# Attention scores in split float32: the low pieces of the keys used where they arise, in matmuls over 64 rows

## The chip, the cores and the metric

The kernel runs on one core of a Trainium2 chip. The metric is the time of one execution in microseconds (us) of device time; three executions of the kernel before took 1040.53, 1043.62 and 1044.70 us, so its median is 1043.62 us. One execution was also recorded by the profiler, instruction by instruction, and all views below are of that record.

## What is computed

One block of a hybrid encoder over 1024 tokens of width 1024, in float32. A normalised input is projected to two groups of heads of 64 columns each. Group A has 8 query heads that share 2 heads of keys and values, a window of 128 tokens with a slope per head (ALiBi) and a learned sink. Group B has 8 heads with keys and values of their own, each chunk of 64 tokens seeing itself and 8 chunks before, with a bias by clipped distance. Then follow norms, an output projection, a residual and an MLP with squared ReLU.

```python
n = rms_norm(h, norm1_g)
qa, ka, va, qb, kb, vb = split(n @ w_in)
# group A, per head
scores = qa @ ka.T * HEAD_DIM ** -0.5 - slopes * dist
p = softmax_with_sink(scores)
ya = p @ va
# group B, per head
scores = qb @ kb.T * HEAD_DIM ** -0.5 + bias[rel]
yb = softmax(scores) @ vb
h = h + concat(rms_norm(ya), rms_norm(yb)) @ w_out
h = h + square(relu(rms_norm(h) @ w_ff1)) @ w_ff2
out = rms_norm(h)
```

## The kernel before

**Two pieces.** TensorE multiplies float32 operands in a rounded form (float32r). To keep precision, each operand x is split into a high piece (x copied to float32r) and a low piece (x minus the high one). A product is the sum of high x high, high x low and low x high (`mm3`, L200).

**Scores.** A head has 64 columns, so a head's high and low queries fit together in the 128 rows of the array. A query tile Q (`new_q`, L462) holds for one head the high piece in rows 0 to 63 and the low piece in rows 64 to 127. Two key tiles go with it (`new_k`, L465: four for the two heads of a pair): one has the high piece of the keys twice, in the upper and the lower 64 rows, the other the low piece twice. So two matmuls over 128 rows give all four products: Q with the high keys, then Q with the low keys, added up in PSUM (`scores`, L598). A block of 128 queries of group A meets 256 columns of keys, in group B 256, 384, 512 or 640 (640 in two parts of 320 in two banks).

**How the pieces get to their rows.** A projection yields both heads of a pair in one tile, head 0 in rows 0 to 63, head 1 in rows 64 to 127. `place` (L350) for group A and `keys_b` (L398) for group B multiply it by the norm's scale on VectorE into a staging tile of the pool `tst` (three buffers), copy it to the high piece on ScalarE, and take the low piece on GpSimd (`split_l`, L176; on VectorE for the first three projections). Then SyncE issues copies from SBUF to SBUF: for queries one for each piece and head, for keys one for each piece, head and repetition (L380 for A, L423 for B). In group B the low pieces are copied first and the copies come once for all 1024 tokens; in group A they come for each 512.

**Stages.** Up to about 40 us the first weights are loaded and the first projections made. Then the units of group A run: scores, exponentials (VectorE adds the bias and finds the maximum, L622, ScalarE takes the exponential, L623), transposes on TensorE (`pt_A`), and the product with the values (`av_A`). From about 160 us the units of group B follow: scores `S_B`, exponentials (L620, L623), pieces in float16 (`H_B`, L863 and L868), a transposing DMA to `G_B` (L871), and float16 matmuls `av_B`. Between the steps of a unit the remaining projections (`ip_qA`, `ip_kB`, `ip_qB`, `ip_vB`) and the output projection of group A (`op_A`) are put in as fillers. Behind about 400 us comes the MLP in float16 pieces, to which nothing here applies.

**What sets the order.** TensorE's order in the attention is the order of the code (`pe`, L136, ties each matmul to the one before; the numbers A_FILL, B_FILL, NEXT_AT and others say how many filler steps go where). On the other engines a scheduler decides from its own estimate of times, so an edit can move instructions that it does not name. SyncE issues nearly all DMAs, one after the other.

Of the kernel before, what the change touches and what calls it, by code (L numbers as in the profile page):

```python
# [12 lines left out]
AF = mybir.ActivationFunctionType  # L13
ALU = mybir.AluOpType
# [3 lines left out]
P = 128  # L18
SEQ = 1024
# [6 lines left out]
HD = 64  # L26
# [32 lines left out]
def kernel(  # L59
# [29 lines left out]
    nc = tc.nc  # L89
# [7 lines left out]
    def f(ap):  # L97
        return ap.bitcast(F32)

    def page(shape, name, dt=F32R):  # L100
        return main.tile(shape, dt, tag="pg", bufs=NPAGES, name=name)
# [68 lines left out]
    def matmul(*args, **kw):  # L170
        pe(nc.tensor.matmul(*args, **kw))  # L171
# [4 lines left out]
    def split_l(engine, lo, full, hi):  # L176
        return engine.tensor_tensor(lo, full, f(hi), ALU.subtract)  # L177
# [85 lines left out]
    R1 = page([P, SEQ], "R1", F32)  # L263
# [86 lines left out]
    def place(acc, kind, name, dst, t, low_engine, st=None, rest=None):  # L350
        if kind == "v" and name != "vA":
            return values_b(acc, name, dst, t)
        if name[1] == "B":
            return keys_b(acc, kind, name, dst, t, low_engine)
        if st is not None:
            pass
        elif name == "vA":
            st = page([P, 2, HALF], f"ts_{name}_{t}")
        else:
            st = main.tile([P, 2, HALF], F32R, tag="tst", bufs=TST, name=f"ts_{name}_{t}")  # L360
        c = slice(t * HALF, (t + 1) * HALF)
        if kind == "v":
            nc.vector.tensor_tensor(f(st[:, 0]), acc, R1[:, c], ALU.mult)
            return lambda *where: turn_v(st, name, dst, t, *where)
        if kind[0] == "q":
            nc.vector.scalar_tensor_tensor(f(st[:, 1]), acc, HD**-0.5, R1[:, c], ALU.mult, ALU.mult)
        else:
            nc.vector.tensor_tensor(f(st[:, 1]), acc, R1[:, c], ALU.mult)
        nc.scalar.activation(st[:, 0], f(st[:, 1]), AF.Copy)
        split_l(low_engine, st[:, 1], f(st[:, 1]), st[:, 0])  # L370

        def copies(heads):
            for hl in range(2):
                for s in heads:
                    src = f(st[s * HD : (s + 1) * HD, hl])
                    if kind == "q":
                        last = nc.sync.dma_start(f(dst[s][hl * HD : (hl + 1) * HD, c]), src)
                    else:
                        for rep in range(2):
                            last = nc.sync.dma_start(f(dst[2 * hl + s][rep * HD : (rep + 1) * HD, c]), src)  # L380
            return last.ins.name

        if rest is None:
            return copies(range(2))
        rest.append(lambda: copies((1,)))
        return copies((0,))

# [5 lines left out]
        nc.scalar.activation(hi, tp, AF.Copy)  # L393
        split_l(nc.vector, dst[t][:, :, :, HD:], tp, hi)

    halves = {}

    def keys_b(acc, kind, name, dst, t, low_engine):  # L398

        if t == 0:  # L400
            halves[name] = [main.tile([P, SEQ], F32R, tag="tst", bufs=TST, name=f"t{hl}_{name}") for hl in (1, 0)]
        c = slice(t * HALF, (t + 1) * HALF)
        lo, hi = (v[:, c] for v in halves[name])
        if kind == "q":
            nc.vector.scalar_tensor_tensor(f(lo), acc, HD**-0.5, R1[:, c], ALU.mult, ALU.mult)
        else:
            nc.vector.tensor_tensor(f(lo), acc, R1[:, c], ALU.mult)  # L407
        nc.scalar.activation(hi, f(lo), AF.Copy)
        split_l(low_engine, lo, f(lo), hi)
        split = name == "qB3"  # L410
        if t == 0 or not split:
            if t == 0 and not split:
                return
            dst.extend(new_q(name) if kind == "q" else new_k(name))
        c = c if split else slice(0, SEQ)
        for hl, v in zip((1, 0), halves[name]):
            for s in range(2):
                src = f(v[s * HD : (s + 1) * HD, c])
                if kind == "q":
                    nc.sync.dma_start(f(dst[s][hl * HD : (hl + 1) * HD, c]), src)  # L420
                else:
                    for rep in range(2):
                        nc.sync.dma_start(f(dst[2 * hl + s][rep * HD : (rep + 1) * HD]), src)  # L423

    def values_b(acc, name, dst, t):

# [35 lines left out]
    def new_q(name):  # L462
        return [page([P, SEQ], f"Q{name}{s}") for s in range(2)]

    def new_k(name):  # L465

        return [page([P, SEQ], f"K{name}{s}") for s in range(4)]

    def new_v(name):
        return [page([P, 4, 2, 2 * HD], f"V{name}{t}") for t in range(2)]  # L470
# [30 lines left out]
    KA, VA, Q = new_k("A"), new_v("A"), new_q("A0")  # L501
# [70 lines left out]
    at = ap_.enter_context(tc.tile_pool(name="at", bufs=1, reuse_waits="tile"))  # L572
# [22 lines left out]
        nb = min(i, 1 if kind == "A" else 4) + 1  # L595
        return i - nb + 1, nb * P

    def scores(kind, i, Q, K, S):  # L598
        k0, n = window(kind, i)
        if n > 512:  # L600
            parts = [(S[:, 0, :320], 0, 320), (S[:, 1, :320], 320, 320)]
        else:
            w = max(n, 2 * P)
            parts = [(S[:, 0, :w], 0, w)]
        for hl in range(2):
            for dst, o, w in parts:
                matmul(
                    dst, Q[:, i * P : (i + 1) * P], K[hl][:, k0 * P + o : k0 * P + o + w],
                    start=hl == 0, stop=hl == 1,
                )  # L610

# [113 lines left out]
    class UnitA:  # L725
# [10 lines left out]
        def score(self, s):  # L736
            p, j = self.pair, self.pair.j
            if s == 0:
                self.nm, self.sm, self.rc = stats(self.name)
            S = group_ps[1].tile([P, 2, 2 * P], F32, tag="S", bufs=2, name=f"S_{self.name}_{s}")  # L740
            pt = tile_of_a(f"P_{self.name}_{s}")
            h = 2 * j + s
            for b in range(2):
                scores("A", self.i0 + b, p.Q[s], p.K[j // 2 :: 2], S[:, b : b + 1])
            for b in range(2):
                c = slice(2 * s + b, 2 * s + b + 1)
                self.P[b, s] = exponentials(
                    "A", self.i0 + b, p.biases()[s], nsink[:, h : h + 1],
                    S[:, b : b + 1], pt[:, b * 2 * P : (b + 1) * 2 * P], self.nm[:, c], self.sm[:, c],
                )  # L750
            if s == 0:
                return
            es = small.tile([P, 4], F32, tag="es", bufs=2, name=f"es_{self.name}")
            for s in range(2):
                c = slice(2 * s, 2 * s + 2)
                nc.scalar.activation(es[:, c], self.nm[:, c], AF.Exp, bias=psink[:, 2 * j + s : 2 * j + s + 1])
            nc.vector.tensor_tensor(self.sm, self.sm, es, ALU.add)
            nc.vector.reciprocal(self.rc, self.sm)
            for (b, s), (k0, n, q) in self.P.items():
                engine = nc.gpsimd if (b, s) in POOL_NORM else nc.vector  # L760
                engine.tensor_scalar(q[:, :n], q[:, :n], self.rc[:, 2 * s + b : 2 * s + b + 1], None, ALU.mult)
# [45 lines left out]
    class UnitB:  # L807
# [10 lines left out]
        def score(self, b):  # L818
            p, h = self.pair, self.h
            if b == 0:  # L820
                self.nm, self.sm, self.rc = stats(self.name)
                banks_of_b()
                pool, cols = (pool_of_b(), 40) if self.t else (at, 20)
                self.G = pool.tile([P, cols, P], F16, tag=f"T16_{self.t}", bufs=2, name=f"G_{self.name}")
            c = slice(b, b + 1)
            S = group_ps[1].tile([P, 2, 512], F32, tag="S", bufs=2, name=f"S_{self.name}_{b}")
            pt = at.tile([P, 5 * P], F32, tag="P", bufs=3, name=f"P_{self.name}_{b}")
            scores("B", self.i0 + b, p.Q[self.s], p.K[self.s :: 2], S)
            if defer:
                defer.pop(0)[1]()  # L830
            self.P[b] = exponentials("B", self.i0 + b, p.biases()[self.s], BIG, S, pt, self.nm[:, c], self.sm[:, c])
            if defer:
                defer.pop(0)[1]()
            if b % 2:
                self.next_bias(b == 1)
            if b % 2:
                H = at.tile([P, 20 * P], F16, tag="P16", bufs=3, name=f"H_{self.name}_{b}")
                defer.append((self, lambda: self.upper(b - 1, H)))
                defer.append((self, lambda: self.lower(b - 1, H)))
# [237 lines left out]
    for j in range(4):  # L1077
        Q, K, V = [], [], []
        fill.add(f"B{j}", in_proj(KB0 + j * P, "k", f"kB{j}", K, None))
        q, v = (QB0 + j * P, "q", f"qB{j}", Q, None), (VB0 + j * P, "v", f"vB{j}", V, None)  # L1080
# [156 lines left out]
    rows = {}  # L1237
# [20 lines left out]
    X, F, S = {}, {}, {}  # L1258
# [402 lines left out]
    acc = {}  # L1661
# [117 lines left out]
    for at, (g, p, n) in enumerate(order2[:-GQ]):  # L1779
# [10 lines left out]
        if g == 0 and step in (4, 7, 10):  # L1790
            last = NQ // GQ - 1
# [21 lines left out]
    g, p, n0 = order2[-GQ]  # L1813
# [104 lines left out]
```

## Time and profile before

| | before |
|---|---|
| median of three executions | 1043.62 us |
| the profiled execution | 1040.53 us |
| its span, first to last instruction | 1038.7 us |
| its mean granted TensorE clock | 0.990 |
| TensorE busy (PE) | 1000.8 us, 4818 matmuls |
| weight loads (PEld) | 591.8 us |
| VectorE (DVE) / ScalarE (ACT) / GpSimd (POOL) busy | 742.5 / 692.6 / 443.9 us |
| DMA | 200.63 MB |

How to read the lines: L171 is line 171 of the kernel; all matmuls have the line of a helper (L171, transposes L174), so they are told apart by the tiles, written out<-in. `128*128` behind a matmul is the part of the array that it uses, `128x512 f32` the shape of its output; `x192` counts instructions. Loads of weights (PEld) overlap matmuls (PE). The end of a matmul is modelled, so the distance from one start to the next says more than a duration. In the lists of waits the numbers are the total in us, how often, and the longest.

### The profile page before, as it was taken

The numbers are of one execution on the slowest core, as the hardware profiler recorded it, in microseconds if no ns is written. First come the engines' busy times: TensorE is split into PE (matmuls) and PEld (weight loads), VectorE is DVE, ScalarE is ACT, GpSimd is POOL, SyncE is SP. The second block draws the span as 40 slices with busy tenths as digits, with TensorE's granted clock in tenths as the row PEclk, the third lists the DMA queues.
The fourth block names the chain that finished last, engine by engine and source line by source line (L and its number), as shares of the span: only waits on it lengthen the run. The fifth ranks groups of instructions, "written<-read, shape, count | busy, mean of one in ns | idle before, by whom it ended". The sixth has DMA issues, their size and how long they took to land.

```text
span 1038.7 us, 14057 instructions
## 1 busy us (share of the span) xinstructions
PE 1000.8 (96%) x4818; PEld 591.8 (57%) x4818; DVE 742.5 (71%) x1259; ACT 692.6 (67%) x1102; POOL 443.9 (43%) x341
## 2 busy tenths in 40 slices
PE   9999999999979999899999999999899999999997
PEld 7878887777757678544444444444344444444443
DVE  6566777867586748994676667664798776786776
ACT  8666766667577736675867865964777765567346
POOL 0456665242453562105245425434255343345333
PEclk9999999999989999989999999999999999999999
DMA  9944438999999885105678668648699545433004
GB/s 353 254 133 133 129 82 184 194 209 225 209 257 251 207 261 182 62 21 166 211 282 293 205 210 274 195 170 310 257 329 388 189 150 186 159 121 122 1 1 162
DMA packets 150567, 200.63 MB, mean 193 GB/s; under 512 B 78688, under 2 KB 96224, under 8 KB 150496
## 3 DMA queue, kind: packets, MB, share of 16 engines
q1 hardware_dynamic: 150352, 199.47, 63.6%
q8 instruction: 38, 0.62, 0.3%
q14 instruction: 33, 0.27, 0.1%
q10 hardware_dynamic: 144, 0.26, 0.1%
HBM read 120.01 MB, written 42.99 MB: 157 GB/s over the span
## 4 chain that ended last, share of the span: by engine, by line
PE 34%; ACT 8%; issue 7%; DMA 7%; DVE 6%; POOL 2%; SPq 1%; DVEq 0%; POOLq 0%; ACTq 0%
PE f_a L171 13%; PE f_c L171 7%; PE f L171 6%; PE f_b L171 4%; DMA w<-in_w_ff_dram 3%; PE op_B L171 2%; ACT w L1362 2%; DMA m<-in_w_ff_dram 2%; DMA u<-ud 2%; POOL W L1397 2%; ACT k L1459 1%; ACT k L1458 1%; ACT W L1395 1%; DMA G_B<-H_B 1%; ACT m L1176 1%
## 5 line engine op out<-in xcount | busy, mean ns | idle before, releaser
L171 PE MATMUL f<-X,W 128*128 128x512 f16 x1344 | 295.3, 381 | 6.6 <-POOL W L1397 5.0
L171 PEld LDWEIGHTS <-U 128*128 128x128 f16 x1356 | 133.0, 98 | 163.9 <-issue 7.2
L171 PEld LDWEIGHTS <-W 128*128 128x128 f16 x1344 | 131.4, 98 | 166.3 <-POOL W L1397 8.2
L1397 POOL TENSOR_TENSOR U<-u,U 128x1024 f16<-128x1024 f32 x48 | 117.3, 2454 | 170.5 <-ACT U L1395 155.2
L171 PE MATMUL f_a<-V,U 128*128 128x512 f16 x756 | 165.3, 379 | 1.0 <-DVE C L1711 1.0
L1397 POOL TENSOR_TENSOR W<-T,W 128x1024 f16<-128x1024 f32 x29 | 69.7, 2407 | 84.3 <-ACT W L1395 84.3
L1397 POOL TENSOR_TENSOR W<-w,W 128x1024 f16<-128x1024 f32 x21 | 51.6, 2458 | 98.6 <-ACT W L1395 98.6
L171 PE MATMUL f_c<-V,U 128*128 128x512 f16 x384 | 86.0, 384 | 3.5 <-DVE V L1399 2.2
L1393 ACT ACTIVATE u<-u,uup 128x1024 f32<-128x1024 f32 x48 | 53.9, 1141 | 53.1 <-DMA u<-ud 53.0
L1399 DVE SCALAR_TENSOR_TENSOR V<-Z,up,V 128x1024 f16<-128x1024 f32 x32 | 51.3, 1605 | 28.7 <-ACT V L1395 20.7
L1395 ACT ACTIVATE U<-u 128x1024 f16<-128x1024 f32 x48 | 50.2, 1046 | 28.1 <-DVE Z L1369 10.4
L623 ACT ACTIVATE P_B<-P_B,nm_B 128x640 f32<-128x640 f32 (+2 forms) x64 | 44.2, 691 | 32.2 <-DVE nm_B L620 16.6
L171 PE MATMUL op_A<-w_o,y 128*128 128x512 f32 x192 | 58.0, 428 | 4.1 <-DVE ts_vB L433 3.9
L868 DVE SCALAR_TENSOR_TENSOR H_B<-P_B,rc_B,H_B 128x640 f16<-128x640 f32 (+2 forms) x64 | 51.0, 825 | 13.6 <-ACT H_B L863 13.3
L1399 DVE SCALAR_TENSOR_TENSOR V<-w,up,V 128x1024 f16<-128x1024 f32 x24 | 42.2, 1756 | 18.0 <-ACT V L1395 13.8
L171 PE MATMUL ip_qB<-nT,w_qB 128*128 128x512 f32 x192 | 53.7, 406 | 1.1 <-DVE t_kB L407 1.0
L171 PE MATMUL ip_kB<-nT,w_kB 128*128 128x512 f32 x192 | 53.7, 405 | 0.0
L1457 DVE CUSTOM_DVE_ANT_0 k<-f,k 128x1024 f32<-128x1024 f32 x24 | 29.3, 1220 | 31.3 <-PE f L171 22.4
L171 PE MATMUL ip_vB<-nT,w_vB 128*128 128x512 f32 x192 | 51.3, 400 | 0.0
L1395 ACT ACTIVATE V<-Z,up 128x1024 f16<-128x1024 f32 x32 | 36.4, 1138 | 22.2 <-DVE Z L1369 19.3
L171 PE MATMUL ip_qA<-nT,w_qA 128*128 128x512 f32 x192 | 50.7, 398 | 0.3 <-DVE VA L177 0.3
L863 ACT ACTIVATE H_B<-P_B,rc_B 128x640 f16<-128x640 f32 (+2 forms) x64 | 40.8, 685 | 9.5 <-DVE rc_B L860 4.2
(284 smaller groups left out, 1980.1 us busy)
## 6 DMA issues: line engine op xcount, KB each, us to landing
w<-in_w_ff_dram SPq DMA_DIRECT2D x64, 512.0 KB, 7.5
u<-ud SPq DMA_DIRECT2D x56, 512.0 KB, 5.4
ud<-k SPq DMA_DIRECT2D x48, 512.0 KB, 3.1
m<-in_w_ff_dram SPq DMA_DIRECT2D x32, 512.0 KB, 5.8
KkB<-t_kB SPq DMA_DIRECT2D x32, 256.0 KB, 5.0
xr<-in_x_dram SPq DMA_DIRECT2D x8, 512.0 KB, 8.8
st_o<-in_w_out_dram SPq DMA_DIRECT2D x8, 512.0 KB, 4.8
h<-in_x_dram SPq DMA_DIRECT2D x8, 512.0 KB, 4.9
```

Of the source, the lines that this page charges most:

```text
L171: pe(nc.tensor.matmul(*args, **kw))
L623: nc.scalar.activation(pr, pr, AF.Exp, bias=nm, scale=-1.0, accum_out=sm)
L863: nc.scalar.activation(hi, q, AF.Copy, scale=rc)
L868: nc.vector.scalar_tensor_tensor(lo, q, rc, hi, ALU.mult, ALU.subtract)
L1176: nc.scalar.activation(src, src, AF.Square, accum_out=self.column())
L1362: nc.scalar.activation(w, w, AF.Copy, scale=up1)
L1393: nc.scalar.activation(full, full, AF.Copy, scale=up)
L1395: nc.scalar.activation(w[0], full, AF.Copy, scale=1.0 if up is None else up)
L1397: engine.tensor_tensor(w[1], full, w[0], ALU.subtract)
L1399: engine.scalar_tensor_tensor(w[1], full, up, w[0], ALU.mult, ALU.subtract)
L1457: dve.tensor_tensor_reduce(v, ps, v, 1.0, 0.0, ALU.add, ALU.max, top)
L1458: nc.scalar.activation(v, v, AF.Relu, scale=down1[n])
```

## The change

The low pieces of the keys are no longer copied. In group A and group B alike the engine that splits writes the low piece straight into a page of its own (`KAl`, `KkB0l` and so on), in which it stands as the projection left it: head 0 (or key head 0) in rows 0 to 63, head 1 in rows 64 to 127. The high pieces are still copied twice for each head. A pair now has three key tiles instead of four (`new_k` returns the low one twice, for the indexing).

The first score matmul stays: 128 rows, queries of both pieces with the high keys. The second is cut to the 64 rows in which the head's low keys lie (`rows` in `scores`, from `half`, which is the key head in group A and the head of the pair in group B). For that the high queries must lie in the same 64 rows: where the half is 1, the query tile now has the low piece in the upper and the high piece in the lower rows (`at = (hl ^ kv) * HD`, `(hl ^ s) * HD`). The product of low queries with low keys is no longer computed. All else stays as it is, the numbers that set the order among it.

```diff
+        hi, raw = st[:, 0], st[:, 1]
+        lo = dst[2][:, c] if kind == "k" else raw
...
+        split_l(low_engine, lo, f(raw), hi)
...
+                if kind == "q":
+                    kv = int(name[2:]) // 2
+                    for hl, src in enumerate((hi, lo)):
+                        at = (hl ^ kv) * HD
+                        last = nc.sync.dma_start(f(dst[s][at : at + HD, c]), f(src[rows]))
+                else:
+                    for rep in range(2):
+                        last = nc.sync.dma_start(f(dst[s][rep * HD : (rep + 1) * HD, c]), f(hi[rows]))
...
-        split_l(low_engine, lo, f(lo), hi)
+        if kind == "k" and t == 0:
+            low_k[name] = page([P, SEQ], f"K{name}l")
+        split_l(low_engine, low_k[name][:, c] if kind == "k" else lo, f(lo), hi)
...
-        for hl, v in zip((1, 0), halves[name]):
+        for hl, v in list(zip((1, 0), halves[name]))[kind == "k" :]:
...
-                        nc.sync.dma_start(f(dst[2 * hl + s][rep * HD : (rep + 1) * HD]), src)
+                        nc.sync.dma_start(f(dst[s][rep * HD : (rep + 1) * HD]), src)
...
-        return [page([P, SEQ], f"K{name}{s}") for s in range(4)]
+        if lo is None:
+            lo = page([P, SEQ], f"K{name}l")
+        return [page([P, SEQ], f"K{name}{s}") for s in range(2)] + [lo, lo]
...
         for hl in range(2):
             for dst, o, w in parts:
+                rows = slice(half * HD, (half + 1) * HD) if hl else slice(0, P)
                 matmul(
-                    dst, Q[:, i * P : (i + 1) * P], K[hl][:, k0 * P + o : k0 * P + o + w],
+                    dst, Q[rows, i * P : (i + 1) * P], K[hl][rows, k0 * P + o : k0 * P + o + w],
                     start=hl == 0, stop=hl == 1,
                 )
```

TensorE's order is the same in both kernels. The first scores of group A, on TensorE, right behind the first projections, stand like this in the kernel before (`KA_197` holds high keys, `KA_199` low ones):

```order
L171 MATMUL ip_vA_427<-nT_192,w_vA 128x512
L171 MATMUL S_A_0_0_592<-KA_197,QA_203 128x256
L171 MATMUL S_A_0_0_592<-KA_199,QA_203 128x256
L171 MATMUL S_A_0_0_592<-KA_197,QA_203 128x256
L171 MATMUL S_A_0_0_592<-KA_199,QA_203 128x256
L171 MATMUL ip_qA_0_611<-nT_181,w_qA_505 128x512
```

The same place on TensorE in the changed kernel, with `KA_198` for the high and `KAl` for the low keys:

```order
L171 MATMUL ip_vA_426<-nT_192,w_vA 128x512
L171 MATMUL S_A_0_0_583<-KA_198,QA_202 128x256
L171 MATMUL S_A_0_0_583<-KAl,QA_202 128x256
L171 MATMUL S_A_0_0_583<-KA_198,QA_202 128x256
L171 MATMUL S_A_0_0_583<-KAl,QA_202 128x256
L171 MATMUL ip_qA_0_602<-nT_181,w_qA_500 128x512
```

Nothing moved; the two matmuls with `KAl` now work on 64 rows, each between two that work on 128.

On SyncE, the queue of DMAs, the key copies of the first pair of group B stand like this before (`KkB_1417` and `KkB_1418` high, `KkB_1419` and `KkB_1420` low; `st_vB` is a weight load, `b_A` a bias, `ya` an output):

```order
L423 DMA KkB_1419<-t_kB_1324 64x1024 x2
L423 DMA KkB_1420<-t_kB_1324 64x1024 x2
L423 DMA KkB_1417<-t_kB_1325 64x1024 x2
L423 DMA KkB_1418<-t_kB_1325 64x1024 x2
L682 DMA ya<-Y_1_1365 128x512
L657 DMA b_A_1699<-in_dist_dram 128x256
L657 DMA b_A_1702<-in_dist_dram 128x256
L127 DMA st_vB_2099<-in_w_in_dram 128x1024
```

The same place on SyncE in the changed kernel, where lines from 382 on have numbers a few higher:

```order
L430 DMA KkB_1409<-t_kB_1316 64x1024 x2
L430 DMA KkB_1410<-t_kB_1316 64x1024 x2
L692 DMA ya<-Y_1_1357 128x512
L127 DMA st_vB_2080<-in_w_in_dram 128x1024
L667 DMA b_A_1685<-in_dist_dram 128x256
L667 DMA b_A_1688<-in_dist_dram 128x256
```

The four low copies are gone, and the weight load stands two places earlier.

On VectorE, in group B where the last projection of values (`ts_vB`) is taken out of PSUM while TensorE goes on to the output projection `op_A`, before:

```order
L405 SCALAR_TENSOR_TENSOR t_qB_3317<-ip_qB_1_3449,R_180 128x512
L917 SCALAR_TENSOR_TENSOR y_1_3403<-y_1_3403,ogc 128x512
L917 SCALAR_TENSOR_TENSOR y_2_3405<-y_2_3405,ogc 128x512
L868 SCALAR_TENSOR_TENSOR H_B_1_1_3490<-P_B_1_0_3458,rc_B_1_3455,H_B_1_1_3490 128x640
L868 SCALAR_TENSOR_TENSOR H_B_1_1_3490<-P_B_1_1_3482,rc_B_1_3455,H_B_1_1_3490 128x640
L620 ISA P_B_1_3_3538,nm_B_1_3453<-S_B_1_3_3537,b_B_587 128x640
L620 ISA nm_B_1_3453 128x1
L917 SCALAR_TENSOR_TENSOR y_3_3407<-y_3_3407,ogc 128x512
L908 TENSOR_TENSOR Y_0_3472<-av_B_0_3494,Y_0_3472 64x512
L433 TENSOR_TENSOR ts_vB_3399<-ip_vB_1_3548,R_180 128x512
```

The same place on VectorE in the changed kernel:

```order
L409 SCALAR_TENSOR_TENSOR t_qB_3288<-ip_qB_1_3420,R_180 128x512
L927 SCALAR_TENSOR_TENSOR y_2_3376<-y_2_3376,ogc 128x512
L927 SCALAR_TENSOR_TENSOR y_3_3378<-y_3_3378,ogc 128x512
L869 TENSOR_SCALAR sm_B_1_3425<-sm_B_1_3425 128x2
L870 RECIPROCAL rc_B_1_3426<-sm_B_1_3425 128x2
L918 TENSOR_TENSOR Y_0_3443<-av_B_0_3465,Y_0_3443 64x512
L878 SCALAR_TENSOR_TENSOR H_B_1_1_3461<-P_B_1_0_3429,rc_B_1_3426,H_B_1_1_3461 128x640
L440 TENSOR_TENSOR ts_vB_3370<-ip_vB_1_3519,R_180 128x512
L878 SCALAR_TENSOR_TENSOR H_B_1_1_3461<-P_B_1_1_3453,rc_B_1_3426,H_B_1_1_3461 128x640
```

`ts_vB` now stands ahead of the second `H_B` and of the score reduction (L620), and behind `Y` as before; on ScalarE `Y` (L907) keeps its place behind `t_qB`, and the two copies that make the high pieces of `H_B` moved behind it.

More of the change, by code (lines that the diff above doesn't have):

```diff
@@ L364, in place @@
             return lambda *where: turn_v(st, name, dst, t, *where)
-        if kind[0] == "q":
-            nc.vector.scalar_tensor_tensor(f(st[:, 1]), acc, HD**-0.5, R1[:, c], ALU.mult, ALU.mult)
-        else:
-            nc.vector.tensor_tensor(f(st[:, 1]), acc, R1[:, c], ALU.mult)
-        nc.scalar.activation(st[:, 0], f(st[:, 1]), AF.Copy)
-        split_l(low_engine, st[:, 1], f(st[:, 1]), st[:, 0])
+        hi, raw = st[:, 0], st[:, 1]
+        lo = dst[2][:, c] if kind == "k" else raw
+        if kind == "q":
+            nc.vector.scalar_tensor_tensor(f(raw), acc, HD**-0.5, R1[:, c], ALU.mult, ALU.mult)
+        else:
+            nc.vector.tensor_tensor(f(raw), acc, R1[:, c], ALU.mult)
+        nc.scalar.activation(hi, f(raw), AF.Copy)
+        split_l(low_engine, lo, f(raw), hi)
         def copies(heads):
[L373 to L380, printed above, removed]
+            for s in heads:
+                rows = slice(s * HD, (s + 1) * HD)
+                if kind == "q":
+                    kv = int(name[2:]) // 2
[5 more added lines that the diff above has]
+                        last = nc.sync.dma_start(f(dst[s][rep * HD : (rep + 1) * HD, c]), f(hi[rows]))
             return last.ins.name
@@ L394, in turn_v @@
         split_l(nc.vector, dst[t][:, :, :, HD:], tp, hi)
-    halves = {}
+    halves, low_k = {}, {}
     def keys_b(acc, kind, name, dst, t, low_engine):
@@ L413, in keys_b @@
                 return
-            dst.extend(new_q(name) if kind == "q" else new_k(name))
+            dst.extend(new_q(name) if kind == "q" else new_k(name, low_k[name]))
         c = c if split else slice(0, SEQ)
-        for hl, v in zip((1, 0), halves[name]):
+        for hl, v in list(zip((1, 0), halves[name]))[kind == "k" :]:
             for s in range(2):
@@ L419, in keys_b @@
                 if kind == "q":
-                    nc.sync.dma_start(f(dst[s][hl * HD : (hl + 1) * HD, c]), src)
+                    at = (hl ^ s) * HD
+                    nc.sync.dma_start(f(dst[s][at : at + HD, c]), src)
                 else:
                     for rep in range(2):
-                        nc.sync.dma_start(f(dst[2 * hl + s][rep * HD : (rep + 1) * HD]), src)
+                        nc.sync.dma_start(f(dst[s][rep * HD : (rep + 1) * HD]), src)
     def values_b(acc, name, dst, t):
@@ L463, in new_q, with new_k @@
         return [page([P, SEQ], f"Q{name}{s}") for s in range(2)]
-    def new_k(name):
-        return [page([P, SEQ], f"K{name}{s}") for s in range(4)]
+    def new_k(name, lo=None):
+        if lo is None:
+            lo = page([P, SEQ], f"K{name}l")
+        return [page([P, SEQ], f"K{name}{s}") for s in range(2)] + [lo, lo]
     def new_v(name):
@@ L596, in window, with scores @@
         return i - nb + 1, nb * P
-    def scores(kind, i, Q, K, S):
+    def scores(kind, i, Q, K, S, half):
         k0, n = window(kind, i)
@@ L743, in score @@
             for b in range(2):
-                scores("A", self.i0 + b, p.Q[s], p.K[j // 2 :: 2], S[:, b : b + 1])
+                scores("A", self.i0 + b, p.Q[s], p.K[j // 2 :: 2], S[:, b : b + 1], j // 2)
             for b in range(2):
@@ L827, in score @@
             pt = at.tile([P, 5 * P], F32, tag="P", bufs=3, name=f"P_{self.name}_{b}")
-            scores("B", self.i0 + b, p.Q[self.s], p.K[self.s :: 2], S)
+            scores("B", self.i0 + b, p.Q[self.s], p.K[self.s :: 2], S, self.s)
             if defer:
```

## The prediction

> **What bounds the kernel now.** I read the page first: who is busy, and in which slices the DMA engines are full.
>
> ```profile
> PE 1000.8 (96%) x4818; PEld 591.8 (57%) x4818; DVE 742.5 (71%) x1259; ACT 692.6 (67%) x1102; POOL 443.9 (43%) x341
> PE   9999999999979999899999999999899999999997
> DMA  9944438999999885105678668648699545433004
> ```
>
> TensorE is busy for 96% of the span. The score matmuls lie between about 40 and 355 us, slices 2 to 14 of 40 (26 us each). In slices 7 to 14 DMA stands at 8 or 9, so copies could matter there. Three windows over this stretch say how much of it TensorE waits.
>
> ```profile
> 60.00:150.00 90.00, 89.97 (x504) 76.50 (x503) 67.09 (x209) 61.75 (x183) 60.57 (x64) 1.00 0.43 118
> 150.00:250.00 100.00, 96.58 (x508) 75.48 (x508) 76.78 (x185) 68.61 (x143) 43.11 (x63) 1.00 0.90 191
> 250.00:360.00 110.00, 102.17 (x503) 74.61 (x502) 80.00 (x172) 77.85 (x152) 46.59 (x50) 0.97 0.98 228
> ```
>
> The columns are the stretch, its length, then PE, PEld, DVE, ACT and POOL busy, clock, DMA share, GB/s. While group A is computed TensorE is idle for 0.03 us of 90. While group B is computed it is idle for 3.4 and 7.8 us, with DMA at 0.90 and 0.98. The waits of TensorE in 150 to 250 (first four) and 250 to 350 us name what ends these gaps.
>
> ```profile
> PE S_B L171 <- DVE nm_B L622: 1.4, 1, 1.4
> PE ip_qB L171 <- DVE t_kB L407: 1.0, 1, 1.0
> PE pt_A L174 <- DVE T_A L177: 0.6, 1, 0.6
> PE av_A L171 <- DVE T_A L177: 0.3, 1, 0.3
> PE op_A L171 <- DVE ts_vB L433: 3.9, 1, 3.9
> PE S_B L171 <- DVE nm_B L620: 3.7, 4, 1.7
> ```
>
> Every one is a wait for VectorE, none for a key copy. So the stretch is bounded by TensorE, then by VectorE's order, and what the change does to a matmul counts nearly one for one.
>
> **Part 1: fewer copies.** Of the key copies half go.
>
> ```profile
> KkB<-t_kB SPq DMA_DIRECT2D x32, 256.0 KB, 5.0
> KA<-ts_kA SPq DMA_DIRECT2D x16, 128.0 KB, 4.8
> ACT t_qB L408 <- DMA KkB<-t_kB: 4.2, 2, 3.5
> SPq L423 <- POOL t_kB L177: 18.5, 3, 14.0
> ```
>
> 16 transfers of 256 KB and 8 of 128 KB are no longer issued. Their relief: ScalarE's two waits for a copy to free the staging tile (4.2 us in all) can go, since that tile is now free as soon as GpSimd has split it. SyncE no longer waits 18.5 us for GpSimd's low pieces, with bias loads, weight loads and transposes queued behind. But no TensorE wait above has a copy at its end. Bounds: nothing, or at most the 11 us of waits listed. I take 0 for the copies, as ScalarE and SyncE have slack here.
>
> **Part 2: the order on VectorE.** The one long gap is the 3.9 us ahead of op_A at 301 to 305 us. It costs more than itself, because the clock falls after it:
>
> ```profile
> 304.00:308.00 4.00, 2.87 (x7) 2.29 (x8) 3.63 (x12) 2.73 (x7) 3.87 (x7) 0.51 1.20 234
> 308.00:312.00 4.00, 4.00 (x17) 2.94 (x16) 2.93 (x5) 2.46 (x5) 3.22 (x5) 0.63 0.87 239
> 300.20 1.67 DVE L868 SCALAR_TENSOR_TENSOR H_B<-P_B,rc_B,H_B 128x640 f16<-128x640 f32 x2
> ...
> 303.67 0.69 DVE L908 TENSOR_TENSOR Y<-av_B,Y 64x512 f32<-64x512 f32 x1 [0.28 <-ACT Y L907]
> 304.38 0.69 DVE L433 TENSOR_TENSOR ts_vB<-ip_vB,R 128x512 f32<-128x512 f32 x1
> ```
>
> At 0.51 and 0.63 the lost work is 0.49 x 2.87 + 0.37 x 4.0 = 2.9 us, so gap and clock are worth 6.8 us. In the changed order (third place shown above) ts_vB stands ahead of the second H_B and the score reduction, but still behind Y, and Y still waits for ScalarE; one H_B now comes between. So it may start some tenths earlier or up to 0.9 us later (one H_B, 1.67 us for two before). Bounds -6.8 to +0.9; I take 0.
>
> The other waits for VectorE (nm_B 1.4 and 3.7, T_A 0.9) shrink if TensorE gets slower, as its results are then due later: -3 us if it does, 0 if not.
>
> **Part 3: the score matmuls over 64 rows.** How many there are, and what one lasts:
>
> ```profile
> L171 PEld LDWEIGHTS S_A<-KA,QqA x96: 187/189/192, 69.5 to 154.7; 128*128 128x128 f32 x96
> L171 PE MATMUL S_A<-KA,QqA x96: 278/282/364, 69.5 to 154.8; 128*128 128x256 f32 x96
> L171 PE MATMUL S_A<-KA,QA x32: 274/282/364, 40.1 to 64.7; 128*128 128x256 f32 x32
> L171 PE MATMUL S_B<-KkB,QqB x192: 277/309/524, 159.8 to 351.8; 128*128 128x320 f32 x128, 128*128 128x256 f32 x32, 128*128 128x384 f32 x16, 128*128 128x512 f32 x16
> ```
>
> Of 128 in A and 192 in B every second one (64 + 96 = 160) becomes a 64-row one, over as many columns as before, so nothing is saved by streaming. The 64 of A stand singly between 128-row ones (hi, lo, hi, lo). In B a row block of up to 512 columns has one low matmul and one of 640 has two together: 64/2 + 128/4 = 64 excursions. Together 128 excursions to 64 rows and back, that is 256 changes of tile size. Every row above has the tile 128*128: no row of this trace shows a change. Its cost is the whole question.
>
> What a matmul costs when its load is hidden, and when it isn't:
>
> ```profile
> 374.45 8.45 PE op_B L171 x36
> 382.91 1.68 PE ss_B L171 x16
> 71.90 0.64 PE L171 MATMUL S_A<-KA,QqA 128*128 128x256 f32 x4
> 72.38 0.86 PE L171 MATMUL ip_qA<-nT,w_qA 128*128 128x512 f32 x3
> ```
>
> 36 matmuls of 512 columns in 8.45 us are 235 ns each, 0.46 ns a column, though each has its own load, and a load of this size lasts 189 ns in the rows above: the loads run beside the streaming. Four S_A take 72.38 - 71.90 = 0.48 us, 120 ns each, and 256 x 0.46 is 118: hidden too. The ss_B matmuls stream one column each, so their 1.68 / 16 = 105 ns is the price of a load with nothing to hide behind.
>
> Below nothing: a hidden load can't be hidden better, 120 against 118 ns, so a gain is excluded. Lower end, the nearest thing to a change of mode, from f32 to f16 and back at the apply matmuls:
>
> ```profile
> 314.99 0.61 PE L171 MATMUL av_B<-G_B,VvB 128*128 128x512 f16 x2
> 315.25 1.05 PE L171 MATMUL op_A<-w_o,y 128*128 128x512 f32 x3
> 316.14 0.50 PE L171 MATMUL av_B<-G_B,VvB 128*128 128x384 f16 x2
> 316.34 0.99 PE L171 MATMUL op_A<-w_o,y 128*128 128x512 f32 x3
> 317.17 0.39 PE L171 MATMUL av_B<-G_B,VvB 128*128 128x256 f16 x2
> 317.17 0.11 PEld L171 LDWEIGHTS <-VvB 128*128 128x128 f16 x2 [0.28 <-issue]
> ```
>
> From av_B to av_B are 1.15 and 1.03 us. Three op_A are 0.705, two av_B of 512 or 384 columns at 0.46 ns are 0.47 or 0.35: the sums, 1.18 and 1.06, even exceed what was measured. The load is held back (0.28 us idle, "issue"), and it costs nothing. So the lower end is 0. Upper end: at each change the matmul before must end (277 - 118 = 159 ns of tail behind its streaming), and only then the load runs (188 ns): 0.35 us, x 256 = 89 us.
>
> Between 0 and 89 us I take the price of an unhidden load, 105 ns a change: weights for another tile size can't be put in place beside a matmul that still uses the whole array, while the tail may overlap the load. 256 x 0.105 = 27 us. This is nearest to the ss_B row, since there too an f32 load of 128 columns has nothing beside it. The f16 row is further off: its array stays 128*128 and its loads are half as long (0.11 us for two). The Trainium skill, TensorEngine Tiling (Array Packing), Tiling Modes, says that changing the tiling mode, not only the tile, drains TensorE; that speaks against this change, and no run here shows it yet. With the 128 cycles of array depth at 2.4 GHz that the Trainium skill, TensorE: Matmul & The Clock Gate, Part 2 (DRAIN), gives, a drain alone would be 53 ns a change, 14 us in all, an estimate from that page; the sum would then be 1054.
>
> **The sum.** The profiled execution took 1040.53 us (span 1038.7); it is the lowest of three, and their median of 1043.62 is 3.1 above. 1040.5 + 27 + 0 + 0 - 3 = 1064.5, on the median 1067.6, given as 1067.
>
> **Rivals.** First, the other side: a change of tile size costs nothing, as that of type does. For it speak the av_B rows; against it, that there the tile stays whole. Then only parts 1 and 2 are left, -6.8 to +0.9, and the median would be about 1042 (1036.8 to 1044.5). It decides from an excursion under (5.2 + 3) / 128 = 64 ns. Second, full serialisation: tail and load in a row at every change, 1043.6 + 89 - 3 = 1130. For it speaks that a reconfigured array may have to be empty before a load; against it, that held-back loads cost nothing at av_B. Halfway between forecast and this lies 1099.
>
> **Chances.** Half a per cent, 5.2 us, is about what can be told from no change here. Forecast 0.49, with its own range 1050 to 1090; free changes 0.31; full serialisation or most of it 0.20. Of the free case a good third, 0.11, has the gap of part 2 closed and is faster by more than 5.2 us; the other 0.20 is no change. All else, 0.69, is slower. The range: down to 1037 takes in nearly all of the free case; up to 1108 half of the serial case. About 0.12 is left out.
>
> **What would show it.** In the changed profile the S rows split into 128*128 and 64*128. Right: an S_A group takes 0.48 + 4 x 0.105 = 0.9 us to the next matmul, PEld shows idle "issue" time ahead of S loads, DMA in slices 7 to 14 falls by some 16 transfers and no TensorE wait for a copy appears. Wrong low: S_A groups still take 0.48 to 0.56 us. Wrong high: S_A groups take 1.5 us or more. Wrong in another way: the time changes behind 400 us, where nothing of this change runs, or the 64-row matmul itself streams slower than 0.46 ns a column.

## The result, and the profile after

The changed kernel took 1081.83 us (median of four executions, 1078.41 to 1083.22) against 1042.07 us before (median of four executions, the three given above among them): 39.8 us more, a ratio of 1.038 with a 95% interval of 1.0357 to 1.0402. Its profiled execution took 1083.22 us with a span of 1081.4, 42.7 us above the span of before.

The page of the changed kernel, the rows that were shown of before:

```profile
PE 1049.8 (97%) x4818; PEld 601.5 (56%) x4818; DVE 744.8 (69%) x1259; ACT 694.5 (64%) x1102; POOL 446.9 (41%) x341
PE   9999999999999999989999998999979999999997
DMA  9833323686999987411676786675799734543004
```

The number of matmuls is the same, and no other engine does clearly more than before: VectorE, ScalarE and GpSimd are busy for 2 to 3 us more. TensorE alone is busy for 49 us more. DMA in slices 3 to 6, with most of group A, falls (3, 3, 3, 2 where 4, 4, 4, 3 stood).

Where TensorE waits, by stages (columns as before: stretch, length, then PE, PEld, DVE, ACT, POOL busy, clock, DMA, GB/s), and its waits in 150 to 400 us:

```profile
60.00:150.00 90.00, 90.00 (x422) 69.15 (x420) 53.72 (x169) 51.83 (x152) 51.15 (x53) 1.00 0.32 85
150.00:250.00 100.00, 97.23 (x434) 68.37 (x434) 69.72 (x183) 60.94 (x143) 39.31 (x45) 0.98 0.60 131
250.00:400.00 150.00, 146.83 (x671) 99.16 (x670) 103.11 (x219) 99.55 (x189) 62.86 (x78) 0.99 0.88 198
```

```profile
PE S_B L171 <- DVE nm_B L632: 2.2, 2, 1.6
PE op_A L171 <- ACT o L1074: 1.7, 1, 1.7
PE ip_qB L171 <- DVE t_kB L411: 0.9, 1, 0.9
PE S_B L171 <- DVE nm_B L630: 0.9, 1, 0.9
PE pt_A L174 <- DVE T_A L177: 0.3, 1, 0.3
```

In the first stage TensorE now does 422 matmuls in 90 us instead of 504, and is busy all the time. The gap of 3.9 us ahead of op_A is gone from the list. So the loss isn't waiting: it sits inside what the profile counts as busy.

The rows of the scores, in the view of the tiles S_A and S_B of the changed kernel:

```profile
L171 PE MATMUL S_A<-KA,QqA x48: 279/373/387, 73.5 to 176.3; 128*128 128x256 f32 x48
L171 PE MATMUL S_A<-KAl,QqA x48: 378/381/383, 73.8 to 176.6; 64*128 64x256 f32 x48
L171 PEld LDWEIGHTS S_A<-KAl,QqA x48: 182/183/183, 73.8 to 176.6; 64*128 64x128 f32 x48
L171 PE MATMUL S_B<-KkB,QqB x96: 276/309/532, 181.4 to 391.7; 128*128 128x320 f32 x64, 128*128 128x256 f32 x16, 128*128 128x384 f32 x8, 128*128 128x512 f32 x8
```

Behind "to" stands the start of the last one. The last S_A started at 154.8 us before and at 176.3 or 176.6 now: 21.8 us later. The last S_B with high keys starts at 391.7; before, the last S_B of all started at 351.8, so some 40 us have come together there. From there to the end only 2 to 3 us are added. Nearly the whole loss arises between the first and the last score, about half in each group.

How, one group of each kind shows. First the timeline of TensorE (start, length as modelled), then its weight loads at the same place:

```profile
73.49 0.36 PE L171 MATMUL S_A<-KA,QqA 128*128 128x256 f32 x1
73.79 0.38 PE L171 MATMUL S_A<-KAl,QqA 64*128 64x256 f32 x1
74.10 0.39 PE L171 MATMUL S_A<-KA,QqA 128*128 128x256 f32 x1
74.41 0.38 PE L171 MATMUL S_A<-KAl,QqA 64*128 64x256 f32 x1
74.72 1.65 PE L171 MATMUL ip_qA<-nT,w_qA 128*128 128x512 f32 x6
...
236.25 0.49 PE L171 MATMUL S_B<-KkB,QqB 128*128 128x512 f32 x1 [1.60 <-DVE nm_B L632]
236.67 0.49 PE L171 MATMUL S_B<-KkB1l,QqB 64*128 64x512 f32 x1
237.09 1.36 PE L171 MATMUL ip_kB<-nT,w_kB 128*128 128x512 f32 x3
```

```profile
73.47 0.19 PEld L171 LDWEIGHTS S_A<-KA,QqA 128*128 128x128 f32 x1
73.78 0.18 PEld L171 LDWEIGHTS S_A<-KAl,QqA 64*128 64x128 f32 x1
74.09 0.19 PEld L171 LDWEIGHTS S_A<-KA,QqA 128*128 128x128 f32 x1
74.41 0.18 PEld L171 LDWEIGHTS S_A<-KAl,QqA 64*128 64x128 f32 x1
```

The four S_A start 0.31 us apart instead of 0.12, and each load starts together with its matmul instead of ahead of it. With 256 columns the step is 0.31 us, with 512 it is 0.42: 0.11 us for 256 columns more, which is their streaming, and a constant of about 0.19 us, which is the length of one load (0.18 to 0.19). So at each change of size the load begins when the streaming before has ended, and lies bare.

### The profile page after: what moved, and what is told of

The parts are those of the page before. It is cut to its first block, busy times and chain, and to the rows that moved or that the text cites. A ratio compares the mean times of both kernels' runs of the same rounds, so it can differ in the third digit from the quotient of the medians.

```text
span 1081.4 us, 14022 instructions
## 1 busy us (share of the span) xinstructions
PE 1049.8 (97%) x4818; PEld 601.5 (56%) x4818; DVE 744.8 (69%) x1259; ACT 694.5 (64%) x1102; POOL 446.9 (41%) x341
## 2 busy tenths in 40 slices
DMA packets 148647, 195.38 MB, mean 181 GB/s; under 512 B 78304, under 2 KB 95840, under 8 KB 148576
## 4 chain that ended last, share of the span: by engine, by line
PE 68%; ACT 10%; DVE 8%; DMA 8%; issue 4%; SPq 1%; POOL 1%; DVEq 0%; ACTq 0%; POOLq 0%
PE f_a L171 13%; PE f L171 7%; PE f_c L171 7%; PE ip_qB L171 4%; PE ip_vB L171 4%; PE ip_kB L171 4%; PE ip_qA L171 4%; PE f_b L171 4%; PE op_A L171 4%; PE S_B L171 4%; DMA w<-in_w_ff_dram 4%; PE S_A L171 3%; PE av_B L171 2%; ACT w L1372 2%; DMA m<-in_w_ff_dram 2%
## 5 line engine op out<-in xcount | busy, mean ns | idle before, releaser
L1409 DVE SCALAR_TENSOR_TENSOR V<-Z,up,V 128x1024 f16<-128x1024 f32 x32 | 48.4, 1511 | 28.3 <-ACT V L1405 18.2
L878 DVE SCALAR_TENSOR_TENSOR H_B<-P_B,rc_B,H_B 128x640 f16<-128x640 f32 (+2 forms) x64 | 49.0, 789 | 16.2 <-ACT H_B L873 15.8
L171 PE MATMUL ip_qB<-nT,w_qB 128*128 128x512 f32 x192 | 56.9, 424 | 0.9 <-DVE t_kB L411 0.9
L171 PE MATMUL ip_kB<-nT,w_kB 128*128 128x512 f32 x192 | 56.7, 422 | 0.0
L633 ACT ACTIVATE P_A<-P_A,nm_A 128x256 f32<-128x256 f32 (+1 forms) x64 | 31.3, 490 | 38.5 <-DVE nm_A L632 37.5
L632 DVE CUSTOM_DVE_ANT_0 P_A<-S_A,b_A,nsink 128x256 f32<-128x256 f32 (+1 forms) x64 | 27.4, 465 | 33.8 <-PE S_A L171 32.1
```

The costliest lines, as they stand in the source:

```text
L632: nc.vector.tensor_tensor_reduce(pr, S[:, 0, :n], bs, -1.0, init, ALU.add, ALU.min, nm)
L633: nc.scalar.activation(pr, pr, AF.Exp, bias=nm, scale=-1.0, accum_out=sm)
L878: nc.vector.scalar_tensor_tensor(lo, q, rc, hi, ALU.mult, ALU.subtract)
L1409: engine.scalar_tensor_tensor(w[1], full, up, w[0], ALU.mult, ALU.subtract)
```

## The experiments

Three theories were tested. Theory 1: a change of tile size holds the next load back. Theory 2: a matmul over 64 rows is itself slow. Theory 3: the moved instructions and the low keys' new path cost the time. The first four kernels were measured together; the kernel before took 1040.38 us beside them. On every engine the instructions of the first and the fourth stand in the order of the changed kernel, those of the second in the order of before. An excursion is a change to 64 rows and back.

**Without the 64 rows.** The edit, in `scores` of the changed kernel:

```diff
-                rows = slice(half * HD, (half + 1) * HD) if hl else slice(0, P)
+                rows = slice(0, P)
```

> The changed kernel with its second score matmul over all 128 rows again, still on the uncopied low keys; copies and the order on every engine are those of the changed kernel. (It adds the low queries of a head times the low keys of the other head, a term of the size of the one that the change leaves out.) Theory 1, a change of tile size holds back the next load, 0.19 us each way: no change of size is left, so the 39.8 us go and the time is 1042 us, within 4 us either way for the fewer copies and the new order. Theory 2, a matmul over 64 rows is itself slow: the same, 1042 us. Theory 3, the moved instructions and the low keys' new path cost the time: it stays near 1082 us.

Measured: 1041.92 us, ratio 1.001 (0.9994 to 1.0027). The whole loss is gone, with half of the key copies gone as well. Theory 3 falls. The tile S_A in this kernel, and its waits of TensorE from 290 to 330 us:

```profile
L171 PE MATMUL S_A<-KAl,QqA x48: 278/281/284, 68.3 to 152.9; 128*128 128x256 f32 x48
```

```profile
PE op_A L171 <- DVE ts_vB L440: 4.3, 1, 4.3
PE op_A L171 <- ACT o L1074: 3.0, 1, 3.0
PE S_B L171 <- DVE nm_B L630: 0.7, 1, 0.7
```

The last S_A starts within 2 us of before. The gap ahead of op_A is 4.3 us, 0.4 more than the 3.9 of before: the new place of ts_vB on VectorE doesn't shorten it. The removed copies and the new order together gain nothing that can be measured; this kernel has both, so a small gain of one and a small loss of the other aren't told apart.

**Only the 64 rows.** The kernel before, copies and all:

```diff
             for dst, o, w in parts:
+                rows = slice(0, HD) if hl else slice(0, P)
                 matmul(
-                    dst, Q[:, i * P : (i + 1) * P], K[hl][:, k0 * P + o : k0 * P + o + w],
+                    dst, Q[rows, i * P : (i + 1) * P], K[hl][rows, k0 * P + o : k0 * P + o + w],
```

> The kernel before with its copies and its order, only the second score matmul cut to rows 0 to 63 (high queries; the product of low queries and low keys is left out). Theory 1: 256 changes of size, so as slow as the changed kernel, 1080 to 1090 us, the start-to-start distances of S_A near 0.31 us instead of 0.12. Theory 2: the same. Theory 3: as fast as before, 1042 us.

Measured: 1077.61 us, ratio 1.0361 (1.0334 to 1.0388), 37.2 us slower (34.7 to 40.4, which takes in the 39.8). This one part makes the loss. Its timeline has the four S_A in one row:

```profile
68.08 1.21 PE L171 MATMUL S_A<-KA,QA 128*128 128x256 f32 x4
69.22 1.65 PE L171 MATMUL ip_qA<-nT,w_qA 128*128 128x512 f32 x6
```

They take 69.22 - 68.08 = 1.14 us, where four took 0.48 before (72.38 - 71.90).

**As many matmuls over 64 rows, fewer changes.** In group A both high matmuls first, then both low ones:

```diff
-    def scores(kind, i, Q, K, S, half):
+    def scores(kind, i, Q, K, S, half, pieces=range(2)):
...
-        for hl in range(2):
+        for hl in pieces:
...
-                    start=hl == 0, stop=hl == 1,
+                    start=hl == 0, stop=hl == 1, skip_group_check=kind == "A",
...
-            for b in range(2):
-                scores("A", self.i0 + b, p.Q[s], p.K[j // 2 :: 2], S[:, b : b + 1], j // 2)
+            for hl in range(2):
+                for b in range(2):
+                    scores("A", self.i0 + b, p.Q[s], p.K[j // 2 :: 2], S[:, b : b + 1], j // 2, (hl,))
```

> The changed kernel with the four score matmuls of a group A step in another order: both high ones, then both low ones over 64 rows. The same 160 matmuls over 64 rows, but group A makes 32 excursions instead of 64, 64 changes of size fewer. Theory 1: 64 x 0.19 = 12 us less than the changed kernel, near 1070 us. Theory 2, the price is per matmul over 64 rows: 1082 us, unchanged. Theory 3: unchanged.

What this kernel computes is no longer the block's result: the sums of two blocks of queries are open in one PSUM bank at the same time, and which part of them is lost was not looked into. Count and size of the matmuls are as the text says. Measured: 1069.14 us, ratio 1.0273 (1.0244 to 1.0302): 28.8 us over before (25.4 to 31.4), where the changed kernel is 39.8 over before (37.2 to 41.9). The 64 changes fewer are worth 11 us by these differences, 12 forecast. Theory 2 wanted no change and falls. In the timeline the second low matmul adds no more than its streaming:

```profile
70.37 0.48 PE L171 MATMUL S_A<-KA,QqA 128*128 128x256 f32 x2
70.78 0.50 PE L171 MATMUL S_A<-KAl,QqA 64*128 64x256 f32 x2
71.21 1.65 PE L171 MATMUL ip_qA<-nT,w_qA 128*128 128x512 f32 x6
```

The two low ones take 0.43 us, 0.12 more than the 0.31 of a single one in the changed kernel; 0.12 us is what 256 columns took before.

**The 64 rows in group B alone.**

```diff
-                rows = slice(half * HD, (half + 1) * HD) if hl else slice(0, P)
+                rows = slice(half * HD, (half + 1) * HD) if hl and kind == "B" else slice(0, P)
```

> The changed kernel with the second score matmul over 64 rows in group B alone; in group A it goes over all 128. 64 of 128 excursions and 96 of 160 matmuls over 64 rows are left. Theory 1: half of the price, 18 to 20 us over the kernel before, near 1061 us. Theory 2: 96/160 of 39.8 is 24 us, near 1066 us. Theory 3: near 1082 us.

Measured: 1056.20 us, ratio 1.0164 (1.0131 to 1.0196), 15.8 us over before. That is 0.25 us for each of 64 excursions; the other 64, in group A, account for the rest, 24 us of 39.8 or 0.37 each. The interval, 13.6 to 20.4 us, takes in the 18 to 20 of theory 1 and leaves out the 24 of theory 2. Half of the excursions cost less than half because group B had waits to give back. TensorE has the same order here as in the first experiment ("Without the 64 rows"), so the steps from one matmul's start to the next can be compared one by one and added up: at the 64 excursions (from the start of the last matmul before the 64 rows to that of the second one behind them) they are 22.9 us longer, idle time not counted; TensorE idles 8.0 us less, and the rest is 1.3 us shorter. That makes 13.6 us, the difference of the two spans (1053.7 and 1040.1).

**Is the price the load, or a fixed time?** In the kernel before the float16 products with the values are cut instead, so that the load on the way in is a short one:

```diff
             for hl in range(2):
+                rows = slice(0, HD) if hl else slice(0, P)
...
-                        self.av[:, c0 : c0 + len(part) * P], p.V[0][:, kb, self.s].rearrange("p a b -> p (a b)"),
-                        self.G[:, where[0] : where[-1] + 1 : d],
+                        self.av[:, c0 : c0 + len(part) * P], p.V[0][rows, kb, self.s].rearrange("p a b -> p (a b)"),
+                        self.G[rows, where[0] : where[-1] + 1 : d],
```

> The kernel before, its scores untouched, but the low matmuls of the float16 product with the values in group B (av_B) cut to rows 0 to 63 (half of each key block is left out of that low product). 96 excursions to 64 rows with a float16 load on the way in (98 ns in the traces) and mostly a float32 load (188 ns) on the way out. Theory 1a, a change of size holds the next load back until the streaming before has ended, and the whole load is the price: 0.098 + 0.188 = 0.29 us an excursion, 28 us, less some 5 us of waits that shrink: about 1065 us. Theory 1b, the price is a fixed 0.19 us for a reconfigured array, whatever is loaded: 0.38 us an excursion, 36 us less 5: about 1073 us. Were only float32 matmuls concerned: 1042 us.

Measured: 1053.27 us against 1040.45 beside it, ratio 1.0128 (1.0103 to 1.0153). The total, 12.8 us, is less than either theory said. The distances tell why. TensorE and its loads in this kernel:

```profile
320.15 0.71 PE L171 MATMUL av_B<-G_B,VvB 128*128 128x512 f16 x2
320.79 0.96 PE L171 MATMUL op_A<-w_o,y 128*128 128x512 f32 x3
321.59 0.71 PE L171 MATMUL av_B<-G_B,VvB 128*128 128x512 f16 x2
```

```profile
320.14 0.10 PEld L171 LDWEIGHTS <-VvB 128*128 128x128 f16 x1 [0.26 <-issue]
320.47 0.09 PEld L171 LDWEIGHTS <-VvB 64*128 64x128 f16 x1 [0.23 <-issue]
320.79 0.53 PEld L171 LDWEIGHTS op_A<-w_o,y 128*128 128x128 f32 x3 [0.23 <-issue]
```

From av_B to av_B are 1.44 us where 1.15 stood before: 0.29 us an excursion, the 0.10 + 0.19 that theory 1a wants, not 0.38. The load to the 64-row matmul starts 0.33 us after the load before it: about 0.10 for that load and 0.23 for streaming 512 columns. What the sum had wrong is the time given back: the row for 250 to 370 us has hardly any idle time left.

```profile
250.00:370.00 120.00, 119.34 (x533) 80.12 (x531) 85.29 (x183) 84.32 (x163) 48.68 (x54) 1.00 0.98 226
```

TensorE is busy for 119.34 of 120 us at clock 1.00, where it stood idle for 7.8 of 110 at 0.97. The same comparison, step by step with the kernel before, closes the sum: the steps at the 96 excursions are 26.3 us longer, 0.27 each, and all others are 14.5 us shorter, 10.4 of it idle time that is gone. 26.3 - 14.5 = 11.8 us, the difference of the two spans (1050.5 and 1038.7). So 14.5 us of idle and slow time were given back instead of 5.

**Size or position?** In the changed kernel the two low matmuls of a 640-column block of group B are put on different halves of the array:

```diff
-                rows = slice(half * HD, (half + 1) * HD) if hl else slice(0, P)
+                at = (half ^ (o > 0)) * HD
+                rows = slice(at, at + HD) if hl else slice(0, P)
```

> The changed kernel, but of the two low matmuls of a 640-column block of group B the second works on the other 64 rows (so its columns get the low keys of the other head with the low queries instead of its own low product). The sizes stay as they are, 256 changes; 32 changes of position inside the pairs come in, into another bank. Theory 1, only the size counts: as the changed kernel, 1082 us; if the two halves of the array work side by side, up to 32 x 0.15 = 5 us less, 1077 us, with the second S_B start right behind the first. Theory 5, any change of the rows in use holds back the load: 32 x 0.19 = 6 us more, 1088 us.

Measured: 1078.06 us, ratio 1.0359 (1.0333 to 1.0384), 37.6 us over its own before, so 1088 is excluded; from the changed kernel's 39.8 it can't be told apart, as the intervals overlap. The rows tell it. TensorE in this kernel, its loads at that place, and then the same group in the changed kernel:

```profile
370.97 0.46 PE L171 MATMUL S_B<-KkB,QqB 128*128 128x320 f32 x2
371.36 0.41 PE L171 MATMUL S_B<-KkB3l,QqB 64*128 64x320 f32 x2
371.70 0.96 PE L171 MATMUL op_A<-w_o,y 128*128 128x512 f32 x3
```

```profile
371.36 0.19 PEld L171 LDWEIGHTS S_B<-KkB3l,QqB 64*128 64x128 f32 x2 [0.19 <-issue]
```

```profile
383.26 0.56 PE L171 MATMUL S_B<-KkB3l,QqB 64*128 64x320 f32 x2
383.75 1.66 PE L171 MATMUL op_A<-w_o,y 128*128 128x512 f32 x6
```

Two low matmuls on different halves take 0.34 us, on the same half 0.49: both loads run together (0.19 us for two), and so do the two matmuls. In these pairs a change of position alone costs nothing; it is the size that counts.

**The gap ahead of op_A.** Two kernels put ts_vB earlier on VectorE, one on top of the first experiment, one on top of the kernel before. The splits of ya and the sums Y are tied behind it by the order of the program (`behind_v`); the edit is the same in both:

```diff
+        ins = nc.vector.tensor_tensor(st[:, t], acc, R1[:, t * HALF : (t + 1) * HALF], ALU.mult)
+        if name == "vB3" and t == 1:
+            turned["v"] = ins.ins.name
...
+            behind_v(nc.vector.tensor_tensor(y, self.av[:HD], y, ALU.add))
...
+            return behind_v(nc.vector.scalar_tensor_tensor(y[:, 1], src, gain, f(y[:, 0]), ALU.mult, ALU.subtract))
```

> The kernel with uncopied low keys and 128 rows in both score matmuls, and on VectorE the eviction of the last values (ts_vB) put ahead of two of the splits of ya and the sum Y that stood before it. It tests the price that the prediction gave to the gap ahead of op_A: 3.9 us and 2.9 us of clock, 6.8 us together. If that price holds and ts_vB starts some 3 us earlier, the gap falls under 2 us, the clock stays up, and the time is 4 to 6 us under the kernel before, 1035 to 1037 us. If TensorE then meets the next wait (op_A for o on ScalarE, S_B for nm_B), less than 2 us are won.

> The kernel before, with all its copies, and the same move of ts_vB on VectorE, here behind both H_B and the score reduction. If the copies have slack, as the prediction took it, this one gains as much as the one without low copies, up to the later place of ts_vB: 2 to 5 us, 1036 to 1039 us. If the fewer copies matter once the gap is smaller, it gains clearly less than that one.

Measured: 1043.01 us, ratio 1.0028 (1.0016 to 1.0041), and 1044.80 us, ratio 1.0039 (1.0024 to 1.0055), against 1040.26 us. Both expectations were wrong: nothing is won, a little is lost. The waits of TensorE around that place, of the first and of the second of these kernels:

```profile
PE S_B L177 <- DVE nm_B L638: 3.4, 1, 3.4
PE op_A L177 <- DVE ts_vB L446: 2.5, 1, 2.5
```

```profile
PE S_B L177 <- DVE nm_B L630: 3.2, 2, 3.0
PE op_A L177 <- DVE ts_vB L439: 1.9, 1, 1.9
```

The gap shrinks to 2.5 and 1.9 us, and the score reduction that was pushed back now makes the next score wait for 3.0 to 3.4 us. In both kernels the new order only moved the wait. That VectorE and ScalarE together bind this place would explain it, but isn't shown. No version measured here beats the kernel before.

## Why the prediction was right, point by point

**TensorE bounds the stretch, and a matmul's cost counts nearly one for one: right in group A, too simple in group B.** In group A, where TensorE stood idle for 1.5 us between 40 and 60 us and for 0.03 in the next 90, 64 excursions (128 loads, 24 us) moved the last score by 21.8 us. In group B the same number gave 15.8 us alone: waits took up a third.

**Copies are worth 0: right.** Without them, in the new order and with full rows the time is that of before (1.001, 0.9994 to 1.0027), though SyncE no longer issues 24 transfers and the DMA engines move 195.38 MB in the changed kernel instead of 200.63. As forecast, no wait of TensorE in the list above ends at a copy. In slices 7 to 10 DMA shows 3, 6, 8, 6 where 8, 9, 9, 9 stood, part of which is only that group B comes some 20 us later.

**The order on VectorE, -6.8 to +0.9, taken as 0: right in value.** With full rows the gap became 0.4 us longer. But the end of -6.8 us was priced too high: in the last two kernels a shorter gap gained nothing. The part of the free case that was to be faster by more than 5.2 us rested on it.

**The price of a change of size, 105 ns: the step that was mis-sized.** The mechanism was as predicted, a load that can't hide. Its size is that of a whole load, 0.19 us: the sum would be 256 x 0.19 = 49 us instead of 27. An S_A group took 1.23 us to the next matmul (73.49 to 74.72; 1.14 in the second experiment), where 0.9 was forecast and 1.5 would have meant full serialisation. The 105 ns came from ss_B, and there the kernel before already showed that loads overlap one another, each 0.19 us long and 16 of them in 1.98 us:

```profile
L171 PEld LDWEIGHTS ss_B<-ones,sqB x16: 187/192/192, 382.5 to 384.3; 128*128 128x128 f32 x16
382.52 1.98 PEld L171 LDWEIGHTS ss_B<-ones,sqB 128*128 128x128 f32 x16
```

So 105 ns is the distance of loads of one size, not the price of one that lies bare; at a change of size they don't overlap. The upper end, 0.35 us with the tail of the matmul before, is excluded: the steps of 0.31 and 0.42 us hold only streaming and load. The lower end, 0 as at the change of type, is excluded by the second kernel. The Trainium skill, TensorEngine Tiling (Array Packing), Tiling Modes, says that a change of mode drains TensorE. The runs agree that it costs, and show what: 0.19 us with a float32 load, 0.10 us with a float16 one. That is the load; no time for a drain shows beside it, where the prediction's estimate of a drain alone was 0.053.

**Waits that shrink, -3 us: too small.** Between 60 and 360 us TensorE stood idle for 0.03 + 3.4 + 7.8 = 11.3 us before; in the changed kernel, between 60 and 400 us, for 2.8 + 3.2 = 6.0. So 5.3 us came back instead of 3, the gap ahead of op_A among them, since TensorE now comes later than VectorE there. 49 - 5.3 = 43.7, and the two spans differ by 42.7. Compared step by step over the whole kernel: 48.0 us more at the 128 excursions (0.375 each, idle time not counted), 6.3 us less idle time, 1.0 us more elsewhere, 42.7 together. The errors have opposite signs, 22 us too little for the load and 2 too little given back, so the second hides a little of the first; that is luck. Against the profiled execution the sum of 1064.5 is 18.7 us low (1083.22), against the median the 1067 is 15 low (1081.83), inside the forecast's own range of 1050 to 1090: 23 us of loss were forecast and 39.8 measured.

**The rivals.** Free changes: excluded. Full serialisation: excluded by the same steps. That the 64-row matmul streams slower, named as a way to be wrong: excluded, 256 columns more take 0.11 us and a second low matmul adds 0.12 us.

## What to carry to other kernels

Count changes of tile size, not matmuls over fewer rows: each one lays the next weight load bare, so put matmuls of one size together, and don't mix sizes between short float32 matmuls on a TensorE that is busy anyway. A term without a row in the trace is better priced at the full duration of what may be exposed (188 ns stood in the rows) than at a throughput from a place where it overlaps itself. And dropping half of the copies of a stage gains nothing if no wait of the bounding engine ends at a copy.

## What the runs showed of the hardware that was not expected

- Two float32 matmuls over 64 rows on different halves of the array, into different PSUM banks, run side by side: 0.34 us for two of 320 columns with their loads, against 0.49 on one half. That agrees with the Trainium skill, TensorEngine Tiling (Array Packing), Tiling Modes, that tiles work independently.
- A change from float32 to float16 and back costs nothing at 128*128, though its load is held back too (0.28 us idle on PEld), while a change to 64 rows with the same float16 load costs its 0.10 us. Why the first stays hidden is left open.
- With 256 columns the product of high queries and low keys over all 128 rows takes 0.12 us, and over 64 rows between two matmuls over 128 it takes 0.31: here, using half of the array is the slower way.
